# Differential attention on one core: the norm's rows three slots later, two gate projections exchanged, squares in one operation, the first head's queries ahead of its keys

## The chip, the cores and the metric

The kernel runs on one core of one Trainium2 chip. A core has TensorE (PE in the profile, its weight loads PEld), VectorE (DVE), ScalarE (ACT), GpSimd (POOL) and SyncE (SP), which here only issues transfers. Each engine works through its own list of instructions in order; they wait for each other by semaphores. The metric is the device time of one execution in microseconds. Before the change it is 3618.62 us, the median of three runs (3608.71 to 3621.73).

## The reference

Two transformer-like blocks are computed on a sequence of 1024 tokens of width 1024, in float32. The change lies in the second block, in its differential attention of 8 heads, whose outcome is normed and multiplied by a sigmoid gate, and in the projections that run beside it (`d_q`, `d_k`, `d_v`, the gated convolution's `c_gate` and `c_val`, and the gates `m_diff`, `m_conv`):

```python
def diff_attention(q, k, v, lq1, lk1, lq2, lk2, norm_g, lambda_init):
    q, k = (a.reshape(bsz, seq, DIFF_HEADS, 2, DIFF_HD) for a in (q, k))
    ...
    def block(args):                       # 128 queries, keys masked by chunks of 64
        s = jnp.einsum('bqhtd,bkhtd->bhtqk', qi, k) * scale
        s = jnp.where(mask, s, -jnp.inf)
        p = jax.nn.softmax(s, axis=-1)
        pd = p[:, :, 0] - lam * p[:, :, 1]  # two softmaxes, one subtracted
        return jnp.einsum('bhqk,bkhv->bqhv', pd, v)
    ...
    o = rms_norm_2(o, norm_g) * (1.0 - lambda_init)
    return o.reshape(bsz, seq, DIFF_HEADS * DIFF_VD)

y = sigmoid(m_conv) * o_conv + sigmoid(m_gla) * o_gla + sigmoid(m_diff) * o_diff
```

## The kernel before

Activations lie with channels on the 128 partitions and the 1024 tokens along the free axis. A float32 product is made of three matmuls of high and low parts (hi·hi, hi·lo, lo·hi), so half of a projection's 512 columns costs 8 x 3 = 24 matmuls of 128x512.

The stage in question is `diff` (differential attention). PE's list is written out by hand there; the other engines' lists, and SP's and POOL's transfers, are put in order by a scheduler. The projections are the carpet: `run` goes through a list of blocks, each a key and a head (`dv` values, `md` the outcome's gate, `cg` and `cv` the convolution's gate and value, `dk` keys, `dq` queries, `mc` the convolution outcome's gate), and each block has two halves of two parts of 12 matmuls. After each part stands a slot, a number that counts up, and whatever `plan` has set down for that slot is issued then: `values` (transposes of v), `scores` of a block of 128 queries (matmuls into `psc`, the maximum `nm` on DVE, the exponentials `e` on ACT), `trans` (transposes `ptr` of the weights), `pv` (the outcome `po`, copied to `o`), `norm_sums` and `norm_rows`. A head has 24 slots (the first 20, having no `md`); the last scores of a head are in its slot 18, and its norm falls into the first slots of the next head. In every slot two of the convolution's 32 steps (`cacc`, L1036 on DVE) are issued with low priority; those of a head's convolution start when its `cv` is there.

The norm works in three parts. `norm_sums` squares `o` on ACT (`osq`), sums it over the partitions with matmuls of one column (`pst`), and then a chain of small DVE operations and one ACT square root gives the factors `rr`. `norm_rows` spreads four of the eight factors into a 128x512 tile (`bc`, L443), PE transposes it into `prow`, and DVE multiplies `o` by it (L1183); after the second half the outcome is multiplied by its gate `sig` (L1186) and written to DRAM (`yd`, on POOL's queue). The tile `bc` has one buffer, which the squares use as well.

Keys and queries need their two halves of 64 partitions moved. The keys: copies of `k0h` and `k0l` into `k1h` and `k1l` (two each), and then one each within `k0h` and `k0l`. The queries: an exchange through a scratch tile in three transfers, each waiting for the one ahead (`swp<-qb`, `qb<-qa`, `qa<-swp`). All of them are issued by SP, which also loads the weights (`raw`); the low part of a weight comes by an adding transfer on POOL's queue (`wlo<-raw`, L388). The first head's `dk` half 0 is done in the stage before, so `run` starts with half 1 of `dk`, then `dq`. Four buffers hold split weights, two hold a projection's sums (`pdn`).

Of the kernel before, what the change touches and what calls it, by code (L numbers as in the profile page):

```python
# [11 lines left out]
F32 = mybir.dt.float32  # L12
# [3 lines left out]
AF = mybir.ActivationFunctionType  # L16
# [4 lines left out]
S = 1024  # L21
D = 1024
P = 128
CT = D // P
H = 512
# [36 lines left out]
MC = 4  # L62
# [221 lines left out]
class Net:  # L284
# [706 lines left out]
    def diff(self, hl, st, pre):  # L991

        nc, tc = self.nc, self.tc
        pool = lambda n, b: st.enter_context(tc.tile_pool(name=n, bufs=b, side="right", reuse_waits="tile"))
        qp, ep, tp, op, cp = pool("dq", 1), pool("de", 2), pool("dt", 1), pool("do", 1), pool("dc", 1)
# [5 lines left out]
        def conv_steps(n):  # L1001
            for _ in range(min(n, len(conv))):
                with tc.high_priority(offset=-LATER):
                    conv.pop(0)()
# [11 lines left out]
        hs_ = lambda half: slice(half * H, half * H + H)  # L1016
# [146 lines left out]
        def norm_sums(h):  # L1163
            x = heads[h]
            pst = self.psT.tile([P, H], F32, tag="T", name="pst")
            for half in range(2):
                sq = op.tile([P, H], F32, tag="bc", name="osq")
                nc.scalar.activation(sq, x.o[:, hs_(half)], AF.Square)
                self.colsum(pst[:, 4 * half:4 * half + 4], sq, self.onef[:, 0:1])
            fac = x.fac  # L1170
            nc.vector.reciprocal(fac, fac)
            ms = self.small.tile([P, 8], F32, tag="ms", name="ms")
            nc.vector.tensor_tensor(ms, pst[:, 0:8], fac, op=ALU.mult)
            nc.vector.tensor_tensor(ms, ms, fac, op=ALU.mult)
            x.r = self.rstd_small(ms, 8, 1.0 / P, EPS)
            nc.vector.scalar_tensor_tensor(x.r, x.r, 1.0 - (0.8 - 0.6 * math.exp(0.0)), fac,
                                           op0=ALU.mult, op1=ALU.mult)
# [11 lines left out]
        events, at = {}, lambda x, f, *a: events.setdefault(x, []).append(lambda: f(*a))  # L1189

        def plan(h, base, pace):

            s = [base + 4 + round(pace * qb) for qb in range(8)]
            for c in range(2):
                at(base + 3 + 2 * c, values, h, c)
            for qb in range(8):
                at(s[qb], scores, h, qb)
                at(s[qb] + 3, trans, h, qb)
                if qb % 2:
                    at(s[qb] + 5, pv, h, qb // 2)  # L1200
            at(s[7] + 7, norm_sums, h)
            at(s[7] + 9, norm_rows, h, 0)
            at(s[7] + 10, norm_rows, h, 1)

        def run(blocks):

            for key, i in blocks:
                if (key, i) not in wts:
                    wts[key, i] = self.w_next(f"{key}{i}")
                for half in ((1,) if (key, i) == ("dk", 0) else (0, 1)):  # L1210
                    ps = self.psB.tile([P, H], F32, tag="B", name="pdn")
                    for k in (0, CT // 2):
                        self.proj_half(ps, wts[key, i], hl, half, range(k, k + CT // 2), k == 0, k > 0)
                        if k:
                            evac[key](i, half, ps)
                        if self.slot >= 0:
                            self.slot += 1
                            for f in events.pop(self.slot, ()):
                                f()
                            conv_steps(2)  # L1220
# [9 lines left out]
        self.w_dma = True  # L1230
        with tc.manual_schedule(engines={nc.tensor.engine}):
            self.slot = -1
            run([("dk", 0), ("dq", 0)])
            self.slot = 0
            base = 0
            for h in range(8):
                blocks = [("dv", h)] + [("md", h)] * (h > 0)
                blocks += ([(k, h + 1) for k in ("cg", "cv", "dk", "dq")] if h < 7 else
                           [("mc", i) for i in range(MC)])
                plan(h, base, (1.5 if h == 0 else 1.7) if h in (0, 7) else 2)  # L1240
                run(blocks)
                base += 4 * len(blocks)
            for x in sorted(events):
                for f in events[x]:
                    f()
# [20 lines left out]
class Ending:  # L1266


    name = side = None
# [30 lines left out]
class Between(Ending):  # L1300
# [3 lines left out]
    name, side = "m2h", "left"  # L1304
# [105 lines left out]
class Final(Ending):  # L1410


    name, side = "fs", "left"
# [93 lines left out]
        self.apply(1, range(5))  # L1507


def mix2_plan(ins):  # L1510
    plan = []
    w = ins["w_in_2"]
    ix = {"dk": 0, "dq": 1, "dv": 2, "cg": 3, "cv": 4, "md": 5}
    order = [("cg", 0), ("cv", 0), ("md", 0)]
    for h in range(8):
        order += [("dk", 0), ("dq", 0)] * (h == 0) + [("dv", h)] + [("md", h)] * (h > 0)
        if h < 7:
            order += [(k, h + 1) for k in ("cg", "cv", "dk", "dq")]
    for k, h in order:
        plan.append((f"{k}{h}", w[6 * h + ix[k]]))  # L1520
    plan += [(f"mc{i}", w[80 + i]) for i in range(MC)]
    plan.append(("f", ins["w_f"]))
    at = lambda g, i: w[48 + 8 * g + i]
    two = {"mc": lambda i: (w[80 + i], w[81 + i]), "qk": lambda g: (at(g, 0), at(g, 1)),
           "gv": lambda g: (at(g, 2), at(g, 3)), "go": lambda j: (at(j // 2, 4 + j % 2), at(j // 2, 6 + j % 2))}
    plan += pair_plan([a for kind, i in PAIRS for a in two[kind](i)])
    plan += [(f"co{i}", ins["w_conv_out"][i]) for i in Gla.ORDER]
    return plan


class Ffn:
# [14 lines left out]
    def pool(self, st, name, bufs, side):  # L1546
        return st.enter_context(self.net.tc.tile_pool(name=name, bufs=bufs, side=side, reuse_waits="tile"))
# [50 lines left out]
    def run(self, st, ending, close=lambda: None):  # L1598

        net, tc = self.net, self.net.tc  # L1600
        ps = st.enter_context(ExitStack())
        ps.enter_context(net.psum(0, 8))
        with tc.manual_schedule(engines=MS(self.nc) | {self.nc.sync.engine}):
            with ExitStack() as s1:
                self.ops(self.pool(s1, "fb1", 1, self.other), ("t2", "t3", "t1", "t4", "b22"))
                last = self.up(s1)
            self.st0.close()
            e = ending(net, st)
            with tc.tile_pool(name="fd", bufs=1, side=self.other, reuse_waits="tile") as dp:
                self.down(dp, last, e)  # L1610
            close()
        e.ps = ps
        return e
# [786 lines left out]
class Gates(Ffn):  # L2400
# [34 lines left out]
    def close(self):  # L2435

        self.st1.close()
        return self.pool(self.st, "gk", 1, "right")
# [272 lines left out]
def pair_plan(aps):  # L2711

    return [(f"su{i}", aps[i]) for i in [0, 1, 2, 4, 3, 5] + list(range(6, len(aps)))]
# [7 lines left out]
def kernel(ctx: ExitStack, tc: tile.TileContext, ins: dict, out: bass.AP, upto=None):  # L2721
# [5 lines left out]
    net.w_plan([(f"o{i}", ins["w_out"][i]) for i in range(8)])  # L2727
    net.w_plan(ffn_plan(ins["w_up"], ins["w_down"], NF1))
    net.w_plan(mix2_plan(ins))
    net.w_plan([(f"o{i}", ins["w_out_2"][i]) for i in range(8)])  # L2730
    net.w_plan(ffn_plan(ins["w_ffn_in"], ins["w_ffn_out"], NF2))
# [135 lines left out]
```

## Time and profile before

| | |
|---|---|
| median of three runs | 3618.62 us |
| profiled execution | 3619.3 us, of it span 3617.5 us |
| PE busy | 3323.9 us (92%) |
| DVE, ACT, POOL busy | 67%, 48%, 45% |
| mean granted TensorE clock | 0.957 of full speed |
| `diff`, first projections to last rows | about 1344 to 2200 us of the span |

PE is the engine with the most to do; what its idle time is and what ended it is read from the view of waits. A matmul's row gives its own length, and matmuls overlap, so what 24 of them cost is read from the times at which rows start. The granted clock is 1.00 at 2.4 GHz and 0.50 at 1.2 GHz.

### The profile page before, as it was taken

The page shows a single profiled execution, that of the slowest core. Times are in us where ns is not written, and L with a number is a line of the kernel's source. Part 1 is how long each engine was busy: PE and PEld are TensorE (multiplying, and loading weights), DVE is VectorE, ACT ScalarE, POOL GpSimd, SP SyncE. Part 2 cuts the span into 40 slices and gives each one's busy share as a digit, 9 for nine tenths or more (in the row PEclk, how much of TensorE's full clock was granted, in tenths as well). Part 3 has the DMA queues.
Part 4 walks back from the last instruction along what each step waited for, and adds up shares of the span by engine and source line. Part 5 has one row for each costly group of instructions (what it writes and reads, how often), then busy time and mean ns, then how long its engine had stood idle before and what let it go on. Part 6 is the DMA issues. An engine that isn't in the chain of part 4 may idle for free. (4 is left out here: it accounts for less than half of the span.)

```text
span 3617.5 us, 42471 instructions
## 1 busy us (share of the span) xinstructions
PE 3323.9 (92%) x15494; PEld 2723.6 (75%) x15494; DVE 2432.3 (67%) x3102; ACT 1738.6 (48%) x2846; POOL 1623.0 (45%) x1147
## 2 busy tenths in 40 slices
PE   8788997999999988899999999999999989999997
PEld 6668885788877876777787776777777768888775
DVE  7888838776677886777767766666477672222777
ACT  6447823444445644545555563545533233333565
POOL 3434307999952340000000015986544087776234
PEclk9889998999999998999999999999999989999998
DMA  3131131222258844333443332433455412222974
GB/s 111 38 105 51 58 117 44 82 82 88 82 175 219 194 105 114 96 97 91 102 99 96 88 84 75 151 131 117 164 210 192 143 50 88 82 82 83 283 173 110
DMA packets 134865, 411.55 MB, mean 114 GB/s; under 512 B 16800, under 2 KB 17184, under 8 KB 134656
## 3 DMA queue, kind: packets, MB, share of 16 engines
q1 hardware_dynamic: 92144, 297.58, 24.9%
q0 software_dynamic: 35456, 86.35, 11.9%
q10 hardware_dynamic: 7056, 24.91, 1.7%
q8 instruction: 122, 2.00, 0.2%
q14 instruction: 87, 0.71, 0.1%
HBM read 232.25 MB, written 84.97 MB: 88 GB/s over the span
## 5 line engine op out<-in xcount | busy, mean ns | idle before, releaser
L398 PE MATMUL pdn<-h,whi 128*128 128x512 f32 x1664 | 540.1, 406 | 3.6 <-DVE k0l L381 2.6
L381 POOL TENSOR_TENSOR wlo<-raw,whi 128x512 fp32r<-128x512 f32 (+1 forms) x217 | 347.6, 1614 | 273.1 <-ACT whi L380 271.3
L1550 DVE TENSOR_TENSOR f<-pf,f 128x512 f32<-128x512 f32 x224 | 154.0, 689 | 363.0 <-PE pf L398 362.5
L398 PEld LDWEIGHTS pdn<-h,whi 128*128 128x128 f32 x1664 | 314.5, 195 | 65.1 <-DVE k0l L381 3.0
L398 PE MATMUL pdn<-h,wlo 128*128 128x512 f32 x832 | 332.7, 400 | 0.0
L1036 DVE SCALAR_TENSOR_TENSOR cacc<-cu,vec,cacc 128x1024 f32<-128x1024 f32 x240 | 307.2, 1280 | 17.2 <-ACT cacc L1034 14.3
L388 POOL DMA_DIRECT2D wlo<-raw x49 | 42.4, 865 | 569.0 <-ACT wlo L387 511.9
L398 PE MATMUL pd<-whi 128*128 128x512 f32 x644 | 256.4, 398 | 20.3 <-DVE f L1550 9.7
L398 PE MATMUL pd<-whi,wlo 128*128 128x512 f32 x644 | 257.3, 400 | 16.5 <-DMA wlo<-fs 9.7
L380 ACT CAST whi<-raw 128x512 fp32r<-128x512 f32 (+1 forms) x234 | 156.0, 694 | 231.4 <-PE pf L398 169.2
L398 PE MATMUL pd<-wlo,whi 128*128 128x512 f32 x644 | 254.3, 395 | 0.0
L380 ACT CAST whi<-sb 128x512 fp32r<-128x512 f32 x128 | 79.1, 620 | 339.4 <-PE pf L398 251.0
L381 POOL TENSOR_TENSOR wlo<-sb,whi 128x512 fp32r<-128x512 f32 x128 | 174.1, 1364 | 105.7 <-ACT whi L380 105.4
L381 POOL TENSOR_TENSOR wlo<-sa,whi 128x1024 fp32r<-128x1024 f32 x64 | 178.2, 2785 | 55.3 <-ACT whi L380 55.2
L398 PE MATMUL pf<-h,whi 128*128 128x512 f32 x576 | 183.5, 400 | 8.9 <-ACT a L2477 4.0
L398 PEld LDWEIGHTS pdn<-h,wlo 128*128 128x128 f32 x832 | 161.0, 193 | 36.4
L398 PE MATMUL pp<-h,whi 128*128 128x512 f32 x448 | 149.8, 415 | 23.4 <-ACT h L534 9.7
L388 POOL DMA_DIRECT2D wlo<-fs x92 | 79.8, 870 | 193.5 <-ACT wlo L387 145.3
L398 PEld LDWEIGHTS pd<-whi,wlo 128*128 128x128 f32 x644 | 123.0, 191 | 52.7 <-DMA wlo<-fs 15.3
L398 PEld LDWEIGHTS pd<-whi 128*128 128x128 f32 x644 | 123.4, 192 | 48.9 <-ACT acc L1883 6.8
L387 ACT ACTIVATE wlo<-whi 128x512 fp32r<-128x512 f32 (+2 forms) x210 | 152.8, 728 | 5.2
L1119 DVE TENSOR_REDUCE nm<-psc 128x1 f32<-128x256 f32 (+7 forms) x128 | 91.1, 751 | 77.4 <-ACT psc L1117 77.0
(565 smaller groups left out, 9747.1 us busy)
## 6 DMA issues: line engine op xcount, KB each, us to landing
raw<-in_w_in_dram SPq DMA_DIRECT2D x102, 512.0 KB, 3.6
raw<-in_w_up_dram SPq DMA_DIRECT2D x48, 512.0 KB, 3.5
wlo<-raw POOLq DMA_DIRECT2D x48, 512.0 KB, 4.6
gd<-f ACTq DMA_DIRECT2D x46, 512.0 KB, 2.6
fs<-gd SPq DMA_DIRECT2D x46, 512.0 KB, 6.7
wlo<-fs POOLq DMA_DIRECT2D x92, 256.0 KB, 4.5
raw<-in_w_ffn_in_dram SPq DMA_DIRECT2D x44, 512.0 KB, 3.5
wlo<-s POOLq DMA_DIRECT2D x69, 256.0 KB, 4.0
```

Of the source, the lines that this page charges most:

```text
L380: (copy or self.nc.scalar.copy)(hi, src)
L381: (eng or self.nc.vector).tensor_tensor(lo, src, hi.bitcast(F32), op=ALU.subtract)
L387: nc.scalar.activation(lo, hi.bitcast(F32), AF.Copy, scale=-1.0)
L388: nc.gpsimd.dma_start(lo.bitcast(F32), src, accum_op=ALU.add)
L398: nc.tensor.matmul(out, a, b, start=(first and i == 0), stop=(last and i == n - 1), skip_group_check=cont)
L1036: conv.append(lambda k=k: nc.vector.scalar_tensor_tensor(acc, u[:, k:k + S], cw(k), acc, op0=ALU.mult, op1=ALU.add))
L1119: nc.vector.tensor_reduce(nm, ps[:, 0:nk], axis=mybir.AxisListType.X, op=ALU.max, negate=True)
L1550: e.tensor_tensor(o, x, y, op=op)
```

## The change

Four edits, all in the order of things. The queries' block of the first head goes ahead of its keys' half block. In each head the outcome's gate `md` goes behind the next head's `cg` (in the last head, behind `mc` 0). The two `norm_rows` go from slots 9 and 10 after the last scores to 12 and 13. The squares of `o` are made in one operation of 1024 columns into a tile of the exponentials' buffer `e1` instead of two of 512 into `bc`. The weights' loading order follows the blocks.

```diff
-            for half in range(2):
-                sq = op.tile([P, H], F32, tag="bc", name="osq")
-                nc.scalar.activation(sq, x.o[:, hs_(half)], AF.Square)
-                self.colsum(pst[:, 4 * half:4 * half + 4], sq, self.onef[:, 0:1])
+            sq = ep.tile([P, S], F32, tag="e1", name="osq", bufs=1)
+            nc.scalar.activation(sq, x.o, AF.Square)
+            self.colsum(pst, sq, self.onef[:, 0:1], 8)
...
-            at(s[7] + 9, norm_rows, h, 0)
-            at(s[7] + 10, norm_rows, h, 1)
+            at(s[7] + 12, norm_rows, h, 0)
+            at(s[7] + 13, norm_rows, h, 1)
...
-            run([("dk", 0), ("dq", 0)])
+            run([("dq", 0), ("dk", 0)])
...
-                blocks = [("dv", h)] + [("md", h)] * (h > 0)
-                blocks += ([(k, h + 1) for k in ("cg", "cv", "dk", "dq")] if h < 7 else
-                           [("mc", i) for i in range(MC)])
+                blocks = head_blocks(h)
...
+def head_blocks(h):
+
+    if h < 7:
+        return [("dv", h), ("cg", h + 1)] + [("md", h)] * (h > 0) + [(k, h + 1) for k in ("cv", "dk", "dq")]
+    return [("dv", h), ("mc", 0), ("md", h)] + [("mc", i) for i in range(1, MC)]
```

On PE, at the start of the second head (the norm of the first), the first rows stood in slot 3 ahead of the transposes `pvt` of the values:

```order
 L398 MATMUL pdn<-h_3_10506,whi 128x512 x2
 L398 MATMUL pdn<-h_3_10506,wlo 128x512
-L452 MATMUL prow<-ident,bc 128x128 x4
 L1098 MATMUL pvt<-ident,vf 128x128 x4
 L398 MATMUL pdn<-h_4_10507,whi 128x512 x2
```

They stand in slot 6 now; the second rows, which stood in slot 4 ahead of the first scores, stand in slot 7 ahead of the first transposes `ptr`:

```order
 L398 MATMUL pdn<-h_3_10506,whi 128x512 x2
 L398 MATMUL pdn<-h_3_10506,wlo 128x512
+L452 MATMUL prow<-ident,bc 128x128 x4
 L1141 MATMUL ptr<-ident,e 128x128
 L398 MATMUL pdn<-h_4_10507,whi 128x512 x2
```

So three slots of 12 matmuls more lie between the sums and the first rows. On DVE, which makes the tile `bc` that these rows wait for, the list from the norm's small operations (`rt`, `rr`) to its second `bc` was this at the start of the fifth head:

```order
L425 SCALAR_TENSOR_TENSOR rt<-rv,rr 128x8
L1036 SCALAR_TENSOR_TENSOR cacc<-cu,vec,cacc 128x1024
L426 TENSOR_TENSOR rt<-rt,rr 128x8
L1036 SCALAR_TENSOR_TENSOR cacc<-cu,vec,cacc 128x1024
L427 SCALAR_TENSOR_TENSOR rr<-rt,rr 128x8
L1036 SCALAR_TENSOR_TENSOR cacc<-cu,vec,cacc 128x1024
L1176 SCALAR_TENSOR_TENSOR rr<-rr,fac 128x8
L1036 SCALAR_TENSOR_TENSOR cacc<-cu,vec,cacc 128x1024
L443 COPY bc<-rr 128x512
L1036 SCALAR_TENSOR_TENSOR cacc<-cu,vec,cacc 128x1024
L1183 SCALAR_TENSOR_TENSOR o<-o,vec,prow 128x512
L443 COPY bc<-rr 128x512
```

Now the first `bc` has a values' low part and a maximum ahead of it and two convolution steps less (one of them in the rows shown below, one ahead of them), and between it and the second `bc` stands this:

```order
L1036 SCALAR_TENSOR_TENSOR cacc<-cu,vec,cacc 128x1024 x2
L1119 TENSOR_REDUCE nm<-psc 128x1
L1036 SCALAR_TENSOR_TENSOR cacc<-cu,vec,cacc 128x1024
L1126 RECIPROCAL sm<-sm 128x1
L381 TENSOR_TENSOR vl<-pvt,vh 128x512
L1127 SCALAR_TENSOR_TENSOR sm<-fac,nlam,sm 128x1
L1036 SCALAR_TENSOR_TENSOR cacc<-cu,vec,cacc 128x1024
L1128 SCALAR_TENSOR_TENSOR e<-e,sm 128x128
L1182 SCALAR_TENSOR_TENSOR o<-o,vec,prow 128x512
L443 COPY bc<-rr 128x512
```

The scores' operations of the next head have come in between the two. On SP, at the first head's keys and queries, the list was:

```order
L1064 DMA k1h<-k0h 64x1024
L1065 DMA k1h<-k0h 64x1024
L1064 DMA k1l<-k0l 64x1024
L1065 DMA k1l<-k0l 64x1024
L1066 DMA k0h<-k0h 64x1024
L353 DMA raw<-in_w_in_dram 128x1024
L1066 DMA k0l<-k0l 64x1024
L1008 DMA swp<-qb 64x1024
L353 DMA raw<-in_w_in_dram 128x1024
L1009 DMA qb<-qa 64x1024
L1010 DMA qa<-swp 64x1024
```

and is now:

```order
L1008 DMA swp<-qb 64x1024
L1009 DMA qb<-qa 64x1024
L1064 DMA k1h<-k0h 64x1024
L1065 DMA k1h<-k0h 64x1024
L1010 DMA qa<-swp 64x1024
L1064 DMA k1l<-k0l 64x1024
L1066 DMA k0h<-k0h 64x1024
L1065 DMA k1l<-k0l 64x1024
L353 DMA raw<-in_w_in_dram 128x1024 x2
L1066 DMA k0l<-k0l 64x1024
```

The queries' exchange has gone to the front, the keys' copies are spread behind it, and two weight loads stand ahead of the last of them. Outside of this stage every engine's order is what it was.

## Rows read from the trace of the kernel before

**Rows 1.** Waits of PE, 1340 to 2230 us: total, times, longest.
```profile
PE prow L452 <- DVE bc L443: 48.0, 8, 6.9
PE pst L436 <- ACT osq L1168: 5.8, 8, 0.8
```

**Rows 2.** Timeline, fourth head's norm, then the last head's: start, length, engine, operation, idle before.
```profile
1793.64 0.95 PE L436 MATMUL pst<-onef,osq 128*128 128x1 f32 x8
...
1795.31 1.05 PE L436 MATMUL pst<-onef,osq 128*128 128x1 f32 x8 [0.72 <-ACT osq L1168]
...
1796.40 0.17 DVE L1173 TENSOR_TENSOR ms<-pst,fac 128x8 f32<-128x8 f32 x1 [0.73 <-PE pst L436]
...
1808.25 0.42 DVE L443 COPY bc<-rr 128x512 f32<-128x512 f32 x1
...
1808.81 1.09 PE L452 MATMUL prow<-ident,bc 128*128 128x128 f32 x4 [6.84 <-DVE bc L443]
...
1814.45 0.31 PE L1115 MATMUL psc<-k0h,qa 128*128 128x128 f32 x1
...
2193.89 0.63 PE L452 MATMUL prow<-ident,bc 128*128 128x128 f32 x4 [1.27 <-DVE bc L443]
```

**Rows 3.** Stretches: length, busy us (instructions) by engine, granted clock, DMA share, GB/s.
```profile
1808.80:1812.30 3.50, 3.49 (x13) 3.11 (x14) 3.42 (x5) 0.59 (x1) 0.00 (x0) 0.50 0.01 2
1491.50:1498.50 7.00, 7.00 (x20) 5.70 (x20) 5.28 (x7) 0.73 (x2) 0.00 (x0) 0.52 0.78 196
1800.00:1900.00 100.00, 92.43 (x469) 77.94 (x468) 72.73 (x106) 55.91 (x103) 6.43 (x9) 0.97 0.41 99
```

**Rows 4.** Groups of DVE, 1780 to 1830 us: busy, mean ns, idle before.
```profile
L1036 DVE SCALAR_TENSOR_TENSOR cacc<-cu,vec,cacc 128x1024 f32<-128x1024 f32 x23 | 29.5, 1283 | 0.3
...
L1183 DVE SCALAR_TENSOR_TENSOR o<-o,vec,prow 128x512 f32<-128x512 f32 x2 | 1.5, 748 | 0.8 <-PE prow L452 0.7
...
L381 DVE TENSOR_TENSOR vl<-pvt,vh 128x512 fp32r<-128x512 f32 x2 | 1.4, 683 | 0.0
L1119 DVE TENSOR_REDUCE nm<-psc 128x1 f32<-128x128 f32 (+1 forms) x4 | 1.2, 351 | 1.5 <-ACT psc L1117 1.5
```

**Rows 5.** Timeline, SP's queue at the fifth head's queries.
```profile
1793.23 0.46 SPq L1008 DMA_DIRECT2D swp<-qb  x1
...
1801.58 0.46 SPq L1010 DMA_DIRECT2D qa<-swp  x1
```

**Rows 6.** DMA issues, 1790 to 1806 us: KB each, us to landing.
```profile
qa<-swp SPq DMA_DIRECT2D x1, 256.0 KB, 2.9
```

**Rows 7.** Timeline, first head: its weight, keys, queries, first scores.
```profile
1369.09 0.89 POOL L388 DMA_DIRECT2D wlo<-raw  x1 [11.49 <-ACT wlo L387]
...
1373.71 0.33 SPq L353 DMA_DIRECT2D raw<-in_w_in_dram  x1
...
1381.70 0.82 PE L398 MATMUL pdn<-h,whi 128*128 128x512 f32 x2 [2.56 <-DVE k0l L381]
...
1395.77 0.57 SPq L1066 DMA_DIRECT2D k0l<-k0l  x1
1396.44 0.54 SPq L1008 DMA_DIRECT2D swp<-qb  x1
...
1412.04 0.48 PE L1115 MATMUL psc<-k0h,qa 128*128 128x128 f32 x1 [11.66 <-DMA qa<-swp]
```

**Rows 8.** DMA issues, 1362 to 1415 us.
```profile
k1h<-k0h SPq DMA_DIRECT2D x2, 256.0 KB, 8.3
k1l<-k0l SPq DMA_DIRECT2D x2, 256.0 KB, 8.6
...
k0l<-k0l SPq DMA_DIRECT2D x1, 256.0 KB, 7.4
swp<-qb SPq DMA_DIRECT2D x1, 256.0 KB, 8.0
qb<-qa SPq DMA_DIRECT2D x1, 256.0 KB, 4.5
```

More of the change, by code (lines that the diff above doesn't have):

```diff
@@ L1513, in mix2_plan @@
     ix = {"dk": 0, "dq": 1, "dv": 2, "cg": 3, "cv": 4, "md": 5}
-    order = [("cg", 0), ("cv", 0), ("md", 0)]
+    order = [("cg", 0), ("cv", 0), ("md", 0), ("dk", 0), ("dq", 0)]
     for h in range(8):
-        order += [("dk", 0), ("dq", 0)] * (h == 0) + [("dv", h)] + [("md", h)] * (h > 0)
-        if h < 7:
-            order += [(k, h + 1) for k in ("cg", "cv", "dk", "dq")]
+        order += head_blocks(h)
     for k, h in order:
-        plan.append((f"{k}{h}", w[6 * h + ix[k]]))
-    plan += [(f"mc{i}", w[80 + i]) for i in range(MC)]
+        plan.append((f"{k}{h}", w[80 + h if k == "mc" else 6 * h + ix[k]]))
     plan.append(("f", ins["w_f"]))
```

## The prediction

> **What bounds the kernel now.** I read the view of waits first, for the stage `diff`. PE is busy for 92% of the span, and among what it waits for is the tile `bc`: 48.0 us in 8 waits, the longest 6.9, and 5.8 us in 8 waits for the squares [rows 1]. Then the timeline of one head's norm, to see what such a wait is made of. The last `pst` matmul ends at 1796.36 (1795.31 + 1.05), DVE's small chain starts right behind it, its first `bc` is made at 1808.25, and PE's first row starts at 1808.81 after 6.84 us idle, so PE had stopped at 1801.97 [rows 2]. From 1796.36 to 1801.97 stood two slots of 12 matmuls: 2.8 us a slot, 5.6 us a half projection. That is my ruler below. The chain from `pst` to the end of `bc` takes 12.3 us (1808.67 − 1796.36), and PE has 5.6 us of work for it. Third, the stretches: right behind this wait the granted clock is 0.50 for 3.5 us with PE busy throughout, although the 100 us around it have 0.97 [rows 3]. At 1.2 instead of 2.4 GHz, half of these 3.5 us is lost, 1.75 us. Last, the first head: PE waits 11.66 us at its first scores, ended by the queries' third transfer [rows 7].
>
> So the norm costs PE about 8.6 us a head: a latency that PE can't fill, and not DVE's work, which is busy 73 of 100 us there [rows 3].
>
> **The change part by part.**
>
> *Rows three slots later.* Between `pst` and the first rows PE now has five slots (14.0 us) and the first scores with the transposes around them (I estimate 1.2 us): it arrives 15.2 us after `pst`. DVE's chain of 12.3 us loses two convolution steps of 1.28 us and takes on one `vl` (0.68) and one `nm` (0.35) [rows 4]: 10.8 us. So `bc` is there 4.4 us early, and the wait goes: 48.0 us, less the last head's 1.27 us [rows 2], as there the rows move past slots with hardly any projection left. **−46.7 us.** With it goes the half clock behind it in seven heads: 7 x 1.75 = **−12.2 us**.
>
> *What is late next.* The second `bc`. From the first to the second, DVE's list has four convolution steps (5.13), `vl` (0.68), `nm` (0.35), the `o` product (0.75) [rows 4], the copy itself (0.42 [rows 2]) and three small operations (an estimate, 0.7): 8.0 us, so it is ready 18.8 us after `pst`. PE gets there after one more slot and the first rows, 15.2 + 2.8 + 0.8 = 18.8 us. The margin is nothing; it can also be a gain of nothing or a wait of 3 us (two convolution steps more ahead of it). Behind the waiting rows PE's whole list is queued, above all the `ptr` transposes and the next projection part. I take 0.5 us at each of seven boundaries, nearest to a margin of nothing, and 2 us at the last head's end, where scores and rows come close together: **+5.5 us** (bounds 0 and 24).
>
> *The first scores, no longer behind the rows.* PE reaches them 7 us earlier against the transfers. At the boundary shown, `swp<-qb` is issued at 1793.23 and `qa<-swp` at 1801.58 [rows 5], landing 2.9 us later [rows 6], 1804.5; PE would be there three slots after `pst`, at 1804.8, less the 0.7 us that the squares no longer take [rows 2], and 0.2 us for the `pvt` transposes: 1804.3. That is 0.2 us late, inside the 0.5 us above.
>
> *Squares in one operation.* The second square was always what PE waited for between its two groups of `pst` (0.72 us in the row [rows 2]); in one operation both are done before PE comes. **−5.8 us** [rows 1]. ACT makes as many elements, and its busy share of 56% [rows 3] covers it. The stretch of these one-column matmuls also holds a fallen clock in two of eight heads: 7.0 us at 0.52 in the one shown [rows 3], about 3.4 us lost each. Sixteen such matmuls still stand there, now without the gap; I take half of 6.8, **−3.4 us** (bounds −6.8 and +20.4).
>
> The Trainium skill (TensorE: Matmul & The Clock Gate, section "A second HAM failure mode: psum-queue depth-cycling") says that short idle gaps between groups of matmuls make the clock swing between its levels and that the throughput pays for it. Two of eight heads agree with it; by it alone this term would be −6.8 us, as the gap between the groups goes.
>
> *`md` behind `cg`.* Both halves end in the same kind of sigmoid on ACT, in exchanged slots; ACT's slack hides it. The gate `sig` has its last reader in slot 7 now, and would be overwritten from slot 4 if `md` hadn't moved; now it is from slot 8. The `o` buffer's write to DRAM leaves three slots later, and the next head's first `o` comes four slots (11 us) behind it, against transfers of 3 to 9 us [rows 8]. Nothing for both; if the cover fails, some 2 us a head.
>
> *The first head.* Before, PE did `dk` half 1 and then `dq`: it stopped at 1379.14 and again worked from 1381.70 (idle 2.56, [rows 7]). `dq` half 0 would start two half projections ahead of 1379.14, at 1367.9. But its weight's low part is issued by POOL only at 1369.09, and SP's `raw` that follows it leaves at 1373.71 [rows 7], so I put its landing at 1373.7: a wait of 5.8 us that `dk` half 1 used to cover. With 1.75 us at the half clock behind it, `dq` ends at 1386.6, `dk` at 1392.2, and four slots later PE is at the first scores at 1403.8, 3.4 us later than before (1412.04 − 11.66 = 1400.4). The exchange's first transfer leaves about 6 us earlier than 1396.44. The keys' copies, though, now follow `dk`, and on SP they stand behind `qb<-qa` and `qa<-swp`, the second `k1l` behind a wait of `k0h`, and `k0l` behind two weight loads of 512 KB. With steps of 3 to 8.6 us [rows 8] the last copy lands at between 1404 and 1424, against 1412 now. Bounds −8 and +12; I take **+3 us**, a little over their middle: the keys take the queries' place as what the first scores wait for.
>
> A sentence on the queue by itself: the Trainium skill (DMA: Bandwidth & Descriptors, section "Anatomy of one DMA — SWDGE (gpsimd) path") says that a wait on a semaphore happens on the issuing sequencer before dispatch. The row agrees: `swp` leaves at 1396.44, right behind `k0l` at 1395.77 [rows 7].
>
> *The sum.* −46.7 − 12.2 − 5.8 − 3.4 + 5.5 + 3 = −59.6 us. The profiled execution's own time is 3619.3 us, 0.7 above the median of the three runs: 3619.3 − 59.6 = **3560 us**, with a range of its own of 3540 to 3588 (first head's and second `bc`'s bounds, and half-clock losses).
>
> **The rivals.**
>
> *DVE is late at the second rows, or the first.* For it: a margin of nothing, and on DVE convolution steps fill what PE no longer waits for. Against it: 27% of DVE's time is free there. Price: a wait of 3 us and 1.75 us at the half clock at seven boundaries, 33.3 us in place of 5.5: **3588 us**.
>
> *The clock falls at `pst` in every head.* So far the fall often came anyway a few us later, behind the wait; with that gone it may come at the one-column matmuls. For it: the two heads that show it [rows 3]. Against it: six don't. Price: 8 x 3.4 = 27.2 us against the 3.4 us left in the sum: **3584 us**.
>
> *The other side: SP's queue puts the wait at the first scores.* The exchange of each head's queries is three transfers in a chain on an in-order queue, with keys' copies and weight loads among them. If the third lands some 18 us after `swp` is issued rather than the 11.3 of rows 5 and 6, PE loses at slot 4 what it gained at the rows. That is the point from which it decides: 6.7 us later. Then only the squares' 5.8 us are gained, and the first head's 12 us are lost: 3619.3 + 12 − 5.8 = **3626 us**. For it: in the first head the same three transfers took 8.0, 4.5 and about 3 us [rows 6, 8] under a fuller load of transfers. Against it: at the other heads DMA is busy 41% of the time [rows 3], and nothing on SP has changed there.
>
> **How the numbers follow.** The forecast has a chance of 0.70, the late `bc` 0.14, the clock 0.11, SP's queue 0.05. The range of 3546 to 3590 takes in the first three and leaves out the last and the forecast's outer edge. A difference of 0.5% is 18.1 us, about what a measurement of this kernel can tell from no change: faster means below 3600.5 us. Forecast, late `bc` and clock lie there but for a last 0.01: 0.94. SP's queue at its price is within 0.5%, and beyond it if the chain is longer still: 0.03 and 0.02. So 0.94, 0.04 and 0.02.
>
> **What would show it.** Right: PE's waits no longer have `prow` behind `bc`, but for the last head's 1 to 2 us, nor `pst` behind the squares; the granted clock of a head's stretch is close to 1.00; from one head's `pst` to the next is about 8 us shorter. In the first head a new wait of 5 to 6 us stands at the first `dq` matmuls, ended by `wlo`, and the first scores still wait, ended by `k0l` rather than `qa`. Wrong: waits of several us a head at `psc` for a transfer, at the second `prow` for `bc`, or at `ptr` for DVE; or a clock of 0.5 behind each `pst`.

## The result and the profile after

The changed kernel takes 3558.62 us, the median of 4 runs (3554.89 to 3561.74), against 3614.38 us before (4 runs beside it): a ratio of 0.9844, 95% interval 0.9821 to 0.9868. The forecast was 3560 us. The span of the profiled execution fell from 3617.5 to 3558.0 us. The stage itself, measured from the projection matmul that waits for the last part of `h` (at 1350.73 before and 1354.07 now) to the start of the last `prow`, fell from 843.2 to 782.7 us, by 60.5; the sum of the terms was −59.6.

PE's waits in the stage (1340 to 2180 us; total, times, longest), to be held against [rows 1]:

```profile
PE psc L1116 <- DMA k0l<-k0l: 6.4, 1, 6.4
PE pdn L398 <- DMA wlo<-raw: 5.0, 1, 5.0
PE psc L1115 <- DMA qa<-swp: 5.0, 2, 4.2
...
PE prow L452 <- DVE bc L443: 4.2, 2, 2.9
...
PE psc L1115 <- DMA k0h<-k0h: 3.3, 1, 3.3
```

The 48.0 us at `prow` are 4.2, both waits at the last head, and the wait for the squares is gone. The first head has three waits that it didn't have. The timeline of the fourth head's norm, as in [rows 2]:

```profile
1770.73 1.84 PE L436 MATMUL pst<-onef,osq 128*128 128x1 f32 x16
...
1783.05 0.42 DVE L443 COPY bc<-rr 128x512 f32<-128x512 f32 x1
...
1787.62 0.60 PE L452 MATMUL prow<-ident,bc 128*128 128x128 f32 x4
...
1790.20 0.42 DVE L443 COPY bc<-rr 128x512 f32<-128x512 f32 x1
...
1791.29 0.60 PE L452 MATMUL prow<-ident,bc 128*128 128x128 f32 x4
```

`pst` ends at 1772.57. The first `bc` is ready 10.9 us later (worked out: 10.8), PE comes 15.05 us later (15.2). The second `bc` is ready after 18.05 us (18.8), PE comes after 18.7 (18.8): it is early by 0.7 us, and no second row waits anywhere but at the last head.

Two stretches, columns as in [rows 3]: behind the wait at the second head's first scores for as long as the clock is down, and 100 us that begin in the third head's projections and take in the fourth's norm:

```profile
1508.96:1515.57 6.61, 6.61 (x19) 5.35 (x20) 3.13 (x5) 2.51 (x7) 0.69 (x2) 0.50 0.70 197
...
1700.00:1800.00 100.00, 99.99 (x515) 84.47 (x514) 79.00 (x118) 62.37 (x114) 8.67 (x13) 1.00 0.45 114
```

PE is busy for all of the second, at a granted clock of 1.00, where a like stretch had 92% at 0.97. From one head's `pst` to the next is 89.7 us, 9.5 less than the 99.2 before. From the first head's norm to the last one's, one half clock is left, in the first of these stretches: PE works 6.6 us in it and loses half, 3.3 us. It stands behind this wait; the three transfers that set it are in SP's timeline under it:

```profile
1508.96 0.44 PE L1115 MATMUL psc<-k0h,qa 128*128 128x128 f32 x1 [4.24 <-DMA qa<-swp]
```

```profile
1494.86 0.46 SPq L1008 DMA_DIRECT2D swp<-qb  x1
...
1500.87 0.46 SPq L1009 DMA_DIRECT2D qb<-qa  x1
...
1505.92 0.46 SPq L1010 DMA_DIRECT2D qa<-swp  x1
```

Here the chain took 14.1 us from `swp` to PE's start, not the 11.3 of rows 5 and 6. The first head, to be held against [rows 7]:

```profile
1377.05 0.80 PE L398 MATMUL pdn<-h,wlo 128*128 128x512 f32 x1 [5.04 <-DMA wlo<-raw]
...
1410.36 0.45 PE L1115 MATMUL psc<-k0h,qa 128*128 128x128 f32 x1 [3.29 <-DMA k0h<-k0h]
...
1417.23 0.47 PE L1116 MATMUL psc<-k0l,qa 128*128 128x128 f32 x1 [6.43 <-DMA k0l<-k0l]
```

The weight's low part is waited for (5.04 us, worked out 5.8), and the scores wait for the keys' copies, 3.29 and 6.43 us, in place of the 11.66 us for the queries.

### The profile page after: what moved, and what is told of

Same layout as the page of the kernel before. It is cut to its first block, busy times and chain, and to the rows that moved or that the text cites. A ratio compares the mean times of both kernels' runs of the same rounds, so it can differ in the third digit from the quotient of the medians.

```text
span 3558.0 us, 42484 instructions
## 1 busy us (share of the span) xinstructions
PE 3311.4 (93%) x15494; PEld 2718.3 (76%) x15494; DVE 2422.9 (68%) x3102; ACT 1739.3 (49%) x2838; POOL 1622.4 (46%) x1147
## 5 line engine op out<-in xcount | busy, mean ns | idle before, releaser
L398 PE MATMUL pdn<-h,whi 128*128 128x512 f32 x1664 | 532.7, 402 | 1.0 <-ACT h L486 0.8
L398 PE MATMUL pd<-whi 128*128 128x512 f32 x644 | 258.9, 402 | 22.6 <-DVE f L1551 11.3
L398 PEld LDWEIGHTS pd<-wlo,whi 128*128 128x128 f32 x644 | 124.7, 194 | 26.2
```

The costliest lines, as they stand in the source:

```text
L398: nc.tensor.matmul(out, a, b, start=(first and i == 0), stop=(last and i == n - 1), skip_group_check=cont)
```

## The experiments

Ratios are to the kernel before, run on the same chip. "The stage" is always that stretch of the profiled execution. The rest of the program is the same code in all of these kernels, and took between 2768 and 2782 us of their spans, so whole times carry some us that no edit explains; where less than 10 us matter I go by the stage.

**The rows and the gate projections alone.** The changed kernel, less two of its edits:

```diff
-            sq = ep.tile([P, S], F32, tag="e1", name="osq", bufs=1)
-            nc.scalar.activation(sq, x.o, AF.Square)
-            self.colsum(pst, sq, self.onef[:, 0:1], 8)
+            for half in range(2):
+                sq = op.tile([P, H], F32, tag="bc", name="osq")
+                ...
-            run([("dq", 0), ("dk", 0)])
+            run([("dk", 0), ("dq", 0)])
```

> The rows three slots later with the gate projections exchanged, and nothing else of the change (two squares, first head's keys ahead of its queries as before). Theory (the terms of the prediction): the eight waits of prow for bc go but for the last head's 1 to 4 us, and the half clock behind them with it, -46.7 - 12.2 + 5.5 = -53 us, a ratio of 0.985; the waits of pst for the second square stay at 0.72 us each, 5.8 in all, and so does the first head's 11.7 us. Open: if the gap between the two groups of pst is what makes the clock fall, the fall of some 3.4 us now stands at the pst of several heads (two as before, or all eight, a ratio of 0.990 to 0.992). Rival: the waits go because the squares free bc's buffer or ACT earlier, not because of the slots: then most of the 48 us are still there, and the ratio is over 0.995.

Measured: 3569.04 us, 0.9865 (0.985 to 0.988). The waits at `prow` are gone but for 2.0 us at the last head, so the slots did that, and the rival falls. But the open point went the other way than two of eight: a head takes 92.2 us, not 89.7. PE's timeline and a stretch behind it, in the third head:

```profile
1674.88 0.95 PE L436 MATMUL pst<-onef,osq 128*128 128x1 f32 x8
...
1676.55 1.05 PE L436 MATMUL pst<-onef,osq 128*128 128x1 f32 x8 [0.72 <-ACT osq L1168]
```

```profile
1678.60:1682.00 3.40, 3.40 (x10) 2.60 (x9) 3.37 (x6) 0.17 (x1) 0.00 (x0) 0.53 0.80 163
```

PE is never idle in these 3.4 us, and the clock is at 0.53. It falls so behind `pst` in each of the first seven heads: 1.7 us lost in six, 3.4 in the first. With the 0.72 us of waiting, that is the 2.5 us.

**The squares alone.** The kernel before with only the three lines on `sq` changed, the other way round.

> The squares in one operation alone, everything else as before. Theory: pst no longer waits, -5.8 us; DVE's chain to bc starts as much earlier as PE does, so the 48.0 us of prow waiting stay 48, and one of the two fallen clocks at pst goes (-3.4, 0 to -6.8): -9 us, a ratio of 0.9975. Rival: the end of DVE's chain is set by its convolution steps and not by when pst is done; then PE comes 0.72 us earlier to the same bc, each prow wait grows from 6.84 to about 7.6 us, and the ratio is 1.000.

Measured: 3616.51 us, 0.9997 (0.9988 to 1.0006; 10 runs against 13): no difference. The time is the rival's, and the theory's 0.9975 lies outside of the interval, which leaves a gain of 4.3 us at most. Of the mechanism the profile shows the theory's and not the rival's: the `prow` waits are 6.85 us, not 7.6 (the total is 52.2 because the last head's grew to 4.2), and the stage is 9.8 us shorter, while the rest of the program happened to be 5.7 us longer. But most of the 9.8 us comes from the first two heads, whose clock no longer falls at `pst`; in a later head the period goes only from 99.1 to 98.9 us, though 0.72 us of waiting are gone. The stretch behind a `prow` wait that ended at 1800.19 shows why:

```profile
1800.20:1804.70 4.50, 4.50 (x15) 3.93 (x16) 4.42 (x6) 0.59 (x1) 0.00 (x0) 0.50 0.01 2
```

PE now works 4.5 us at the half clock behind the wait instead of 3.5 [rows 3], which costs 0.5 us: most of the 0.72 goes back there. And this profile is of the execution with the highest granted clock of the ten (0.957; the others have 0.954 to 0.956). The mean of the ten is 0.955, against 0.958 in the 13 runs before; over 3616 us that is an estimated 10 us more lost to the half clock, if PE was busy in it. So the edit alone takes waits away and comes with a lower clock; where in the program that stands in the other nine runs, no trace shows.

**Squares in two operations, without the gap.** The changed kernel with the first head's order of before, and

```diff
-            nc.scalar.activation(sq, x.o, AF.Square)
+            for half in range(2):
+                nc.scalar.activation(sq[:, hs_(half)], x.o[:, hs_(half)], AF.Square)
```

> The changed kernel with the first head's order of before, and its squares in two operations of 512 columns again, but both into the one tile of 1024, ahead of the sixteen pst matmuls. It asks whether it is the gap of 0.72 us between two groups of pst that made the clock fall behind each pst (1.7 us lost a head where the rows had been moved and the squares had not), or the two operations. Theory, the gap: no wait at pst, granted clock 1.00 through the stretch behind it in seven of eight heads, 3557 us. Rival: the clock falls at the one-column matmuls with or without a gap as soon as the squares are done in two; then 1.7 us a head are lost, some 3569 us.

Measured: one run, 3556.58 us. The sixteen matmuls stand in one row, and the clock behind them is 1.00:

```profile
1674.63 1.84 PE L436 MATMUL pst<-onef,osq 128*128 128x1 f32 x16
```

```profile
1674.60:1684.60 10.00, 10.00 (x55) 8.56 (x54) 8.79 (x14) 2.67 (x4) 0.86 (x1) 1.00 0.80 184
```

The heads take 89.7 us. So the gap did it, and the number of operations nothing: what counts is that the second square no longer waits for the first one's matmuls to give its tile free.

**Rows two slots earlier.** The changed kernel with

```diff
-            at(s[7] + 12, norm_rows, h, 0)
-            at(s[7] + 13, norm_rows, h, 1)
+            at(s[7] + 10, norm_rows, h, 0)
+            at(s[7] + 11, norm_rows, h, 1)
```

> The changed kernel with its rows in slots 10 and 11 after the last scores instead of 12 and 13. Theory (the wait is DVE's chain less PE's work ahead of the rows): DVE's list has eight convolution steps and one vl ahead of the first bc, about 11.5 us from the end of pst, and PE comes after three slots and the first scores, 9.6 us: a wait of some 1.5 to 2 us in seven heads, for the second bc none, and nothing or 1.7 us at the half clock behind each: 10 to 25 us slower than the changed kernel, a ratio to before of 0.987 to 0.992. Rival: the waits went for another reason than the slots (the squares' new buffer, ACT earlier); then it is as fast as the changed kernel, 0.9845.

Measured: 3593.06 us, 0.9932 (0.9916 to 0.9949), slower by more than was expected: 32 us above the changed kernel by the two ratios, 26.5 us by the stage. DVE's and PE's timeline in the fourth head:

```profile
1781.67 0.17 DVE L1172 TENSOR_TENSOR ms<-pst,fac 128x8 f32<-128x8 f32 x1 [1.18 <-PE pst L436]
...
1792.84 0.42 DVE L443 COPY bc<-rr 128x512 f32<-128x512 f32 x1
...
1793.41 0.63 PE L452 MATMUL prow<-ident,bc 128*128 128x128 f32 x4 [3.00 <-DVE bc L443]
```

The chain takes 11.6 us (11.5 expected), but PE came 8.8 us after `pst` and not 9.6: in this slot the rows stand ahead of the first scores. The wait is 3.00 us in each of seven heads, 21 us, and in six of them half a clock stands behind it, which loses 1.6 to 3.3 us. The mechanism held; 0.8 us a head and the clock were under-sized.

**The gate projections not exchanged.** The changed kernel with `md` directly behind `dv` in `head_blocks`.

> The changed kernel without the exchange of the two gate projections (md of a head directly behind its values, as before). Theory: the tile of the gate has one buffer, so the sigmoid of md's first half, due in slot 6, waits on ACT until DVE has multiplied the outcome by the old gate, which now is in slot 7 or 8; ACT's list stands still for 3 to 7 us and with it the exponentials of the next head, so PE waits 2 to 6 us at the transposes ptr or at the next scores in seven heads, with a half clock behind some: 15 to 50 us slower than the changed kernel. Rival: ACT's slack hides it, and the exchange is worth nothing (within 5 us of the changed kernel).

Measured: one run, 3585.36 us. DVE's, ACT's and PE's timeline in the fourth head:

```profile
1800.58 1.22 DVE L1185 TENSOR_TENSOR o<-o,sig 128x1024 f32<-128x1024 f32 x1
...
1802.88 1.08 ACT L1044 ACTIVATE sig<-pdn 128x512 f32<-128x512 f32 x2
...
1803.53 0.73 PE L398 MATMUL pdn<-h,whi 128*128 128x512 f32 x2 [2.23 <-ACT sig L1044]
```

The price is in the theory's range and not in its place: PE waits 2.2 to 2.8 us in six heads, but for the projection's sum buffer `pdn`, which the gate's sigmoid reads, not at the transposes; a head takes 92.3 us. The stage is 18.5 us longer than in the changed kernel. The cause is shown in part. At the second head, where PE doesn't wait, the sigmoid starts when the old gate has been read (1525.43, right behind the read's end at 1525.40). In the six heads where PE waits, it stands on ACT behind a weight's cast and a table load (1.28 us) and starts 1.1 to 2.0 us after that read. That the scheduler put it there for the old gate's sake is likely, but not shown.

**The convolution steps left out.** The kernel before with

```diff
-                for k in range(30):
+                for k in range(0):
                     conv.append(lambda k=k: nc.vector.scalar_tensor_tensor(
```

> The kernel before with the 30 convolution steps of each head on DVE left out (so cvd holds only the first tap). It asks what the 12.3 us between pst and bc are made of. Theory: nine convolution steps of 1.28 us stand between the eight small operations in DVE's list; without them the chain takes some 3 to 4 us, PE needs 5.6 us to get to the rows where they stood before, the waits of prow for bc go but for 1 to 2 us at the last head, and so does the half clock behind them: 55 to 60 us less than before, the same as the rows' move. Rival: the chain is the latency of its own links (DVE to ACT's square root with its table load, and back); then it still takes 8 us or more and 2 to 3 us of waiting a head are left.

Measured: one run, 3557.85 us. DVE's timeline of the whole chain:

```profile
1762.27 0.17 DVE L1173 TENSOR_TENSOR ms<-pst,fac 128x8 f32<-128x8 f32 x1 [3.24 <-PE pst L436]
...
1763.12 0.20 DVE L423 RECIPROCAL rr<-rr 128x8 f32<-128x8 f32 x1 [0.28 <-ACT rr L422]
...
1763.96 0.17 DVE L1176 SCALAR_TENSOR_TENSOR rr<-rr,fac 128x8 f32<-128x8 f32 x1
1764.16 0.43 DVE L443 COPY bc<-rr 128x512 f32<-128x512 f32 x1
```

It takes 2.4 us, less still than the 3 to 4 expected. Ten of the 12.3 us before were convolution steps that had been put between the links of a chain that PE waited for. The `prow` waits go here as well (2.0 us left), with the rows where they had been. With the squares still in two groups, the clock falls for 3.4 us behind `pst` in the first seven heads, as it did with the rows alone.

**The first head's order.** The changed kernel with `run([("dk", 0), ("dq", 0)])`, run twice; the second time beside the changed kernel.

> The changed kernel with the first head's order of before (keys, then queries). Theory: the first head's exchange cost about 2 to 3 us net (5.0 at the weight, 3.3 and 6.4 at the first scores against 2.6 and 11.7), so this one is 2 to 3 us faster than the changed kernel, 0.1% and hardly outside of the noise; in the profile the first pst comes 2 us earlier against the stage's start, one wait of 11 to 15 us at the first scores ends with qa, and the wait of 4.2 us at the second head's first scores stays. Rival: queries first is what keeps the transfers out of each other's way; then the first scores wait 15 us or more here and this kernel is 2 us or more slower than the changed one.

> The changed kernel with the first head's order of before once more, on the same chip as the candidate, to compare the two: 3557 us by its first runs. If the candidate's gain is real, the two differ by 9 to 12 us, 0.3%; if the packing takes it back, by less than 3.

> The changed kernel again beside these, for the price of the first head's new order: theory 2.6 us slower than with the old order (its first pst came 150.6 us into the stage, against 148.0), at the edge of what the runs can tell; the first head's waits are 5.0 at the weight, 3.3 and 6.4 at the first scores.

Measured: 3557.46 us (0.9834, 0.982 to 0.9849) and 3558.67 us (0.9833, 0.982 to 0.9847); the changed kernel beside the second 3559.05 us (0.9842, 0.9829 to 0.9856). From the stage's first matmul to the first `pst` it is 137.7 and 140.0 us with the old order, 140.0 and 138.7 with the new one. The theory of 2.6 us rested on one profile of each and falls. Over all profiles here but the one without convolution steps and the one with later scores, the old order has 137.1 to 140.0 (six, mean 138.2) and the new one 138.7 to 140.1 (five, mean 139.5): if the exchange costs anything it is about 1 us, which the whole times can't tell from nothing. The wait for `qa` was 12.3 and 14.2 us here, so two profiles of one kernel differ by as much as the two orders.

**Queries ahead of keys in every head.** The changed kernel with `("cv", "dq", "dk")` in `head_blocks`.

> The changed kernel with queries ahead of keys in every head, not only in the first. Theory: the three chained transfers of the queries have four slots (11 us) more, the keys' copies, only two deep, need some 6 to 8 us of the 11 us that they have; the waits for qa at the second head (4.2 us and half a clock behind it, 2.0) and at a later one (0.7) go: -7 us against the changed kernel, a ratio of 0.983 against before. Rival: what the first head shows happens in every head, the keys' copies stand behind waits of the exchange on SP's queue, the first scores wait some 3 to 6 us for k0l in seven heads, and with the half clock behind them that is +20 to +50 us against the changed kernel (0.990 to 0.998).

Measured: 3580.84 us, 0.9896 (0.9879 to 0.9914). The rival held, with smaller waits than its 3 to 6 us. PE's waits:

```profile
PE psc L1116 <- DMA k0l<-k0l: 23.7, 8, 6.5
...
PE psc L1115 <- DMA k0h<-k0h: 3.7, 3, 2.7
```

No wait for `qa` is left, and the keys' last copy is waited for in all eight heads, 1.3 to 4.1 us outside of the first.

**A version that beats both.** The changed kernel with the first head's order of before, and

```diff
-            s = [base + 4 + round(pace * qb) for qb in range(8)]
+            s = [base + (6 if h < 2 else 4) + round((1.43, 1.7, pace)[min(h, 2)] * qb) for qb in range(8)]
```

> A candidate: the changed kernel with the first head's order of before, and the first two heads' scores begun in slot 6 instead of 4 (first head at a pace of 1.43 slots instead of 1.5, second head at 1.7 instead of 2). Theory: the 12.3 us for the queries in the first head become some 6.7, the 5.3 us in the second head none, with the half clock behind it (1.7 to 2) gone, less 1 to 2 us for more scores in neighbouring slots that wait for ACT: -9 to -12 us against the same kernel without it, 3546 to 3549 us. Rival: the scores that are packed closer wait for ACT's exponentials by as much as is gained (2.2 us at each pair of neighbouring slots): no gain.

Measured: 3550.36 us, 0.9812 (0.9799 to 0.9826), 8.3 us under the same kernel without it on the same chip, a little less than the 9 to 12 expected; the stage is 11 to 14 us shorter. The wait at the first scores:

```profile
1412.74 0.47 PE L1115 MATMUL psc<-k0h,qa 128*128 128x128 f32 x1 [6.03 <-DMA qa<-swp]
```

It was 12.3 and 14.2 us; the second head has none. A new one of 2.4 us for `qa`, with 1.7 us lost to the clock, came up at the third head.

## Why the prediction was right

By its own terms, each against the stage:

- *Rows:* −46.7 worked out. In seven heads exactly this went; the rows two slots earlier show that the slots did it. What the kernel without convolution steps corrects is the prediction's "a latency that PE can't fill, and not DVE's work": the chain's own links take 2.4 us, and the other ten were DVE's work, put between them. That DVE has time to spare in all (busy 73 of 100 us) doesn't help an operation behind others in its list.
- *Last head's rows:* +2 in the term of the second `bc`. The wait grew from 1.27 to 4.2 us. The rows alone leave 2.0 there, the squares alone 4.2, so the growth comes with the squares. It is the same fault again: with the squares in one operation, six operations of the next part (`g`) stand between the links in DVE's list, where two stood before.
- *Half clock behind the rows:* −12.2, from 3.5 us in one head. Over the seven heads PE had worked 3.0 to 4.9 us at the half clock behind the wait, 26.5 in all, so −13.2. Between the first and the last norm no half clock is left but the one behind `qa`.
- *Second `bc`:* +3.5 in the seven heads; measured 0. The margin was 0.7 us, not nothing.
- *First scores:* inside that 0.5 us a head. Measured 4.24 us at the second head with 3.3 us lost at the half clock behind it, and 0.73 us at a later head: 8.3 us. This is the mechanism of the rival on SP's queue, in one head of seven; the step took the chain of one boundary, 11.3 us, for all. The trace of the kernel before already had a longer one at its second head: the third transfer landed at 1502.4 (1499.41 + 3.0), 12.4 us after `swp` was issued. `pst` ended there at 1492.39, so by the prediction's own ruler (8.4 − 0.7 + 0.2 us from `pst` to the first scores at the full clock) PE would come at 1500.3, 2.1 us too early.
- *Squares:* −5.8 for the waits and −3.4 for the clock at `pst`. Measured −5.8 and −6.8: neither of the two heads falls there now. (The last head fell there too, for 3.4 us; it is in no term.) The term came out on the right side, but its reasoning was too weak. The rival that the clock would fall at `pst` in every head was real, as the kernel with the rows alone shows; it was this edit that took it away. The −6.8 rest on one profile of each kernel. So the edit is worth 10 to 12 us once the rows are moved (3569.04 against 3557.46 and 3558.67), and nothing that can be measured without: that is shown by whole times.
- *`md`:* nothing, with 2 us a head if the cover failed. The kernel without the exchange paid 2.2 to 2.8 us in six heads. The slots given were wrong: the gate is written from slot 6 and now from slot 10, not 4 and 8.
- *First head:* +3. Measured +1.5 between the two profiles (138.5 to 140.0), about +1 over all profiles. (Four slots of 2.8 us behind 1392.2 are 1403.4, not 1403.8; nothing hangs on it.) The waits that were foretold came (5.0 at the weight, 9.7 at the keys), and sum to about what they replaced (14.8 us against 14.2).

The last head's rows in the profile after, and SP's timeline at the second head in the kernel before:

```profile
2130.09 2.21 DVE L1551 TENSOR_TENSOR g<-g,g 128x512 f32<-128x512 f32 x3
...
2134.39 1.08 PE L452 MATMUL prow<-ident,bc 128*128 128x128 f32 x4 [2.94 <-DVE bc L443]
```

```profile
1490.02 0.46 SPq L1008 DMA_DIRECT2D swp<-qb  x1
...
1499.41 0.46 SPq L1010 DMA_DIRECT2D qa<-swp  x1
```

With these, −46.7 + 2.9 − 13.2 − 5.8 − 6.8 + 8.3 + 1.5 = −59.8 against −60.5 measured (the clock at the last head's end is in none of the terms). That the sum lay so near is partly luck: the waits for `qa` cost 4.8 us more than the +3.5 that had been put on `bc`, and the clock at `pst` (−6.8 for −3.4), the clock behind the rows and the first head gave 5.9 us more than was forecast.

Two things stay open. Why the second head's exchange takes 14 us and the others' 10 to 12 was not tried. A weight load of SP stands between the transfers in every head; but in the second head it is issued ahead of `qb<-qa` and POOL's `wlo` ahead of `swp<-qb`, and in the next heads each behind it, and there `swp` lands after 2.9 us, in the second head after 5.7. And before the change the same gap of 0.72 us at `pst` went with a fallen clock in three heads only (the first two and the last); that it goes with one in seven heads when the rows no longer wait is shown by two kernels, its reason is not.

## What to carry to other kernels

When PE waits for a chain of small operations, look at what the scheduler has put between its links: here ten of twelve us were work of low priority, and either moving the consumer by the chain's length or clearing the chain takes the wait away. Set the consumer by counting both sides from the same event (10.9 us of chain against 15.05 of PE work), the second consumer too, and price the half clock behind a wait along with it: two slots less cost about 30 us, 21 of waiting and the clock on most of it. Take such a count at every boundary and not at one: the second head's transfers were slower than those of the head that was read. And test edits together: two that look independent can share a loss, so that one alone shows nothing and both show all.

## What the runs showed of the hardware

A gap of 0.72 us between two groups of eight one-column matmuls goes with a granted clock near 0.50 for 3.4 us or more behind it, while PE is busy without a break: in seven heads of eight in the two kernels whose rows no longer wait, in three of eight in the kernel before. The same sixteen without the gap leave it at 1.00. Behind waits for `bc` of 3.00 us the clock fell in six heads of seven, for 3.4 us or for 6.8, and in one not at all.
